# State-space output products of four heads in four column groups, and one unread transpose behind the last

## The chip, the core and the metric

The kernel runs on one core of a Trainium2 chip. The metric is the device time of one execution in microseconds; the time before is the median of three runs. The engines are called by their short names in the rows: PE (TensorE matmul), PEld (TensorE weight load), DVE (VectorE), ACT (ScalarE), POOL (GpSimd), SP (SyncE, which issues most transfers).

## The reference

One decoder layer on 256 tokens of width 2048, in float32. A wide projection feeds sliding-window attention, a diagonal state-space branch and two sigmoid gates; the branches are merged, projected, and followed by a gated feed-forward with a short convolution. The change lies in the state-space branch, whose core is this:

```python
bu = einsum('gph,blgh->blgp', bb, ug)             # complex, 32 groups of 16 channels, 64 states
xs = associative_scan(combine, (ab, bu), axis=1)  # over the 256 tokens
y = (einsum('ghp,blgp->blgh', c_re, xs_re) - einsum('ghp,blgp->blgh', c_im, xs_im)
     + d_skip.reshape(SSM_GROUPS, SSM_GROUP) * ug)
y_val, y_gate = split(gelu(y) @ w_glu + b_glu, 2)
ssm = y_val * sigmoid(y_gate)
```

The two einsums of `y` are the output products of the title.

## The kernel before

Activations stand transposed: channels on the partitions, 256 tokens along the free dimension. All large weights come as units of 128 x 1024 numbers. Each unit is cast by ScalarE into a rounded part `whi`, VectorE subtracts to get the rest `wlo`, and TensorE makes three products of each 128 x 128 block (hi by hi, hi by the activation's rest, lo by hi). The main loop (from line 995) goes through the units in a fixed order: q, u, kv, the gates ga and gs, the attention's output product A, glu, S, the output projection o, then up and dn of the feed-forward. Five units are prepared ahead (`LOOK`), in five buffers.

The attention (`g_attn`, line 631) and the state-space branch (`g_ssm`, line 372) are generators that are woven into this loop. They yield for a VectorE turn ("D") or a ScalarE turn ("A"), or until something is there. `later(fn)` (line 757) puts TensorE work aside until the planner's clock of TensorE, `clk_pe`, has passed a due time; `run_aux` (line 765) issues it between two blocks of the main loop. The planner's clocks are sums of modelled costs (lines 92 to 120); they set the order of the instructions only, and what runs when is then set by semaphores on the chip.

The state-space branch has 16 turns j (`NJ`), each for two groups with 64 states: 128 partitions. They are called heads here; four of them make one block c of 128 output channels. In turn j:

- `va`, `vb` (line 583): VectorE takes the input products `pq[j]` from PSUM and turns them by the powers `E`;
- `products` (line 593) issues on TensorE `y_mm(j - 1, x)`, the output products of the head before, and `pq_mm(j + 1)`, the input products of the next;
- `Z` (line 601): four scans on VectorE;
- `xa`, `xb` (line 617): the states turned back, into `x`, which TensorE reads as float32;
- once in four turns `y_ev(c - 1)` (line 568) adds the skip term and writes the block back into `uY`.

`y_mm` (line 560) makes two products of one head: the stationary `cT` is 128 x 32, so each head uses one column group of 32 columns of the array, and writes 32 partitions of the bank `yps[c]`. A float32 matmul leaves two records in the trace, so a head leaves four. The tile pool gives `T1`, `T2` and `Z` two buffers each, `Sc` and `PT` of the attention one each. After the last head, `g_act` (line 711) applies gelu to `uY` and splits it into `su`, the moving operand of glu; between the two units of glu0 the main loop issues A3x and A3y, the last blocks of the attention's output product. E is built at lines 457 to 501 with work tiles under the tags `T1` and `T2`, by VectorE and, for the last doubling, ScalarE.

Of the kernel before, what the change touches and what calls it, by code (L numbers as in the profile page):

```python
# [8 lines left out]
F32 = mybir.dt.float32  # L9
# [3 lines left out]
ALU = mybir.AluOpType  # L13
AX = mybir.AxisListType

P = 128
T = 256
# [120 lines left out]
def hybrid_block_kernel(  # L138
# [33 lines left out]
    def bank(tag, *dims):  # L172
        banks[0] += 1
        return axp.tile([P, *dims], F32, tag=tag, name=f"{tag}{banks[0]}", bufs=2 if tag == "at" else 1)
# [197 lines left out]
    def g_ssm():  # L372
# [86 lines left out]
        V.memset(E[:, 1, :, 0:1], 0.0)  # L459
        V.tensor_copy(E[:, 0, :, 1:2], cn.unsqueeze(2))  # L460
        V.tensor_copy(E[:, 1, :, 1:2], sn.unsqueeze(2))
        L = 1
        while L < P:
            cnt = L if L < 64 else 63
            jn = min(NJ, 256 // L) if L < 64 else 2
            late = []
            for j0 in range(0, NJ, jn):
                js = slice(j0, j0 + jn)
                a = p1.tile([P, 2, jn, cnt], F32, tag="T1", name=f"ea{L}_{j0}", bufs=2)
                b = p1.tile([P, 2, jn, cnt], F32, tag="T2", name=f"eb{L}_{j0}", bufs=2)  # L470
                lr = E[:, 0:1, js, L : L + 1].to_broadcast([P, 2, jn, cnt])
                li = E[:, 1:2, js, L : L + 1].to_broadcast([P, 2, jn, cnt])
                src = E[:, :, js, 1 : cnt + 1]

                def add(js=js, a=a, b=b):
                    tt(E[:, 0, js, L + 1 : L + 1 + cnt], a[:, 0], b[:, 1], ALU.subtract)
                    tt(E[:, 1, js, L + 1 : L + 1 + cnt], a[:, 1], b[:, 0], ALU.add)

                if L == 64 and j0 // jn % 3 == 2:
                    yield "D", None  # L480
                    tt(a, src, lr, ALU.mult)
                    tt(b, src, li, ALU.mult)
                    add()
                elif L == 64:
                    yield "A", None
                    for j in range(jn):
                        S.activation(a[:, :, j], src[:, :, j], AF.Identity, scale=E[:, 0, j0 + j, L : L + 1])
                        S.activation(b[:, :, j], src[:, :, j], AF.Identity, scale=E[:, 1, j0 + j, L : L + 1])
                    late.append(add)
                    if len(late) == 2:  # L490
                        yield "D", None
                        late.pop(0)()
                else:
                    tt(a, src, lr, ALU.mult)
                    tt(b, src, li, ALU.mult)
                    add()
                    if L >= 8:
                        yield "D", None
            for f in late:
                yield "D", None  # L500
                f()
            L *= 2
# [9 lines left out]
        def z3(a):  # L512
            return a.unsqueeze(2).to_broadcast([P, NJ, 32])

        wa = p1.tile([P, NJ, 32], F32, tag="T1", name="cwa", bufs=2)
        wb = p1.tile([P, NJ, 32], F32, tag="T2", name="cwb", bufs=2)
        tt(wa, cT[:, 0], z3(zi), ALU.mult)
        tt(wb, cT[:, 1], z3(zi), ALU.mult)
        tt(cT[:, 0], cT[:, 0], z3(zr), ALU.mult)
# [37 lines left out]
                    PE.matmul(pq[j][:, ri], B[c][h][rows, i % 2, P * ri : P * ri + P], U[c][rows, i % 2], start=h == 0,  # L557
                              stop=h == 1, tile_position=(r, 0))

        def y_mm(j, x):  # L560
            c, i = j // 4, j % 4
            if i == 0:
                yps[c] = bank("yp", T)
            o = yps[c][32 * i : 32 * i + 32]
            PE.matmul(o, cT[:, 0, j], x[:, 0], start=True, stop=False, tile_position=(0, 32 * i))
            PE.matmul(o, cT[:, 1, j], x[:, 1], start=False, stop=True, tile_position=(0, 32 * i))

        def y_ev(c):
            stt(uY[:, c], uY[:, c], pcol("d", c), yps[c], ALU.mult, ALU.add)
# [10 lines left out]
        for j in range(NJ):  # L580
            c = j // 4
            yield "D", tok
            a = p1.tile([P, 2, 2, P], F32, tag="T1", name=f"va{j}", bufs=2)
            b = p1.tile([P, 2, 2, P], F32, tag="T2", name=f"vb{j}", bufs=2)
            tt(a, pq[j], bE(0, j), ALU.mult)
            tt(b, pq[j], bE(1, j), ALU.mult)
            tt(a[:, 0], a[:, 0], b[:, 1], ALU.add)
            tt(a[:, 1], a[:, 1], b[:, 0], ALU.subtract)
            if j % 4 == 3 and c < 3:
                yield "A", None  # L590
                split_b(c + 1)

            def products(j=j, x=x):
                if j:
                    y_mm(j - 1, x)
                if j + 1 < NJ:
                    pq_mm(j + 1)

            tok = later(products)
            yield "D", None  # L600
            Z = p1.tile([P, 2, 2, P], F32, tag="Z", name=f"z{j}", bufs=2)
            ini = p1.tile([P, 4], F32, tag="ini", name=f"ini{j}", bufs=2)
            mb = mag[:, j : j + 1].to_broadcast([P, P])
            for ri in range(2):
                V.tensor_tensor_scan(Z[:, ri, 0], mb, a[:, ri, 0], 0.0, op0=ALU.mult, op1=ALU.add)
            ts(ini[:, 2:4], Z[:, :, 0, 127], E128[:, 0, j : j + 1], ALU.mult)
            stt(ini[:, 0:1], Z[:, 1, 0, 127:128], E128[:, 2, j : j + 1], ini[:, 2:3], ALU.mult, ALU.add)
            stt(ini[:, 1:2], Z[:, 0, 0, 127:128], E128[:, 1, j : j + 1], ini[:, 3:4], ALU.mult, ALU.add)
            for ri in range(2):
                V.tensor_tensor_scan(Z[:, ri, 1], mb, a[:, ri, 1], ini[:, ri : ri + 1], op0=ALU.mult, op1=ALU.add)  # L610
            if j % 4 == 1 and c < 3:
                yield "A", None
                stage_u(c + 1)
            yield "D", tok
            if j % 4 == 2 and c < 3:
                load_b(c + 1)
            x = p1.tile([P, 2, 2, P], F32, tag="T1", name=f"xa{j}", bufs=2)
            b = p1.tile([P, 2, 2, P], F32, tag="T2", name=f"xb{j}", bufs=2)
            tt(x, Z, bE(0, j), ALU.mult)
            tt(b, Z, bE(1, j), ALU.mult)  # L620
            tt(x[:, 0], x[:, 0], b[:, 1], ALU.subtract)
            tt(x[:, 1], x[:, 1], b[:, 0], ALU.add)
            if j % 4 == 0 and j:
                y_ev(c - 1)
                st[f"y{c - 1}"] = True
        yield "D", later(lambda: y_mm(NJ - 1, x))
        y_ev(3)
        st["y3"] = True

# [1 line left out]
    def g_attn():  # L631
# [40 lines left out]
        for i in range(8):  # L672
            if i == 4:
                yield "A", wait_for("q1")
            yield "D", later(lambda: scores(i))
            Sc = p1.tile([P, 2, 3, P], F32, tag="Sc", name=f"sc{i}")
            n6 = p1.tile([P, 2, 3], F32, tag="n6", name=f"n6_{i}", bufs=2)
            nm = p1.tile([P, 2, 2], F32, tag="nm", name=f"nm{i}", bufs=2)
            sm = p1.tile([P, 2, 2], F32, tag="sm", name=f"sm{i}", bufs=2)
            es = p1.tile([P, 2, 2], F32, tag="es", name=f"es{i}", bufs=2)  # L680
            nsb = nsink[:, 2 * i : 2 * i + 2].unsqueeze(2).to_broadcast([P, 2, 2])
            for h in range(2):
                V.scalar_tensor_tensor(out=Sc[:, h], in0=dist.rearrange("p (s k) -> p s k", s=3),
                                       scalar=-SLOPES[i + 8 * h], in1=ps[h], op0=ALU.mult, op1=ALU.add)
            V.tensor_reduce(n6, Sc, AX.X, ALU.max, negate=True)
            V.tensor_tensor(n6[:, :, 1:2], n6[:, :, 1:2], n6[:, :, 2:3], op=ALU.min)
            V.tensor_tensor(nm, n6[:, :, 0:2], nsb, op=ALU.min)
            V.tensor_tensor(es, nm, nsb, op=ALU.subtract)
            yield "A", None
            for h in range(2):  # L690
                S.activation(Sc[:, h, 0], Sc[:, h, 0], AF.Exp, bias=nm[:, h, 0:1], accum_out=sm[:, h, 0:1])
                S.activation(Sc[:, h, 1:3], Sc[:, h, 1:3], AF.Exp, bias=nm[:, h, 1:2], accum_out=sm[:, h, 1:2])
            S.activation(es, es, AF.Exp)
            yield "D", None
            V.tensor_tensor(sm, sm, es, op=ALU.add)
            V.reciprocal(sm, sm)
            yield "A", None
            for h in range(2):
                S.activation(Sc[:, h, 0], Sc[:, h, 0], AF.Identity, scale=sm[:, h, 0:1])
                S.activation(Sc[:, h, 1:3], Sc[:, h, 1:3], AF.Identity, scale=sm[:, h, 1:2])  # L700
            yield "A", later(lambda: turn(Sc))
            PT = p1.tile([P, 2, 3, P], F32, tag="PT", name=f"pt{i}")
            for h in range(2):
                S.copy(PT[:, h], ps[h])
            yield "A", later(lambda: values(PT))
            S.copy(ath[:, i], ps[0])
            yield "D", None
            V.tensor_tensor(atl[:, i], ps[0], ath[:, i].bitcast(F32), op=ALU.subtract)
# [509 lines left out]
```

## Time and profile before

| | us |
|---|---|
| runs: lowest, median, highest | 1214.19, 1214.31, 1218.68 |
| profiled execution | 1220.22 |
| its span, first to last instruction | 1218.4 |
| TensorE busy in the span | 1204.8 |
| VectorE busy | 825.9 |
| ScalarE busy | 600.2 |
| mean granted clock of TensorE | 0.996 |

The time of the profiled execution is its span and 1.8 us around it. Matmuls are pipelined and the ends of their records are modelled, so their busy time is not work at full rate; the distance from one start to the next says more. A row of the chain gives the time from the end of one step to the end of the next.

### The profile page before, as it was taken

How to read it: one execution, taken by the hardware profiler on the slowest of the kernel's cores; microseconds unless marked ns; L12 is line 12 of the kernel's file. 1: busy time of each engine (PE TensorE's matmuls, PEld its weight loads, DVE VectorE, ACT ScalarE, POOL GpSimd, SP SyncE). 2: the span in 40 equal slices, each digit the busy share in tenths (PEclk: the TensorE clock that was granted, in tenths of full speed). 3: DMA queues.
4: the chain of work that ended last, by engine and by line, in shares of the span. 5: the costliest groups of instructions: out<-in, count | busy, mean ns of one | idle time of the engine just before them, and what ended most of it. 6: DMA issues, size and time to landing. Idle time of an engine off the chain costs nothing.

```text
span 1218.4 us, 24557 instructions
## 1 busy us (share of the span) xinstructions
PE 1204.8 (99%) x10348; PEld 1181.8 (97%) x10348; DVE 825.9 (68%) x1172; ACT 600.2 (49%) x817; POOL 10.4 (1%) x24
## 2 busy tenths in 40 slices
PE   9999999999999999999999999999999999999996
PEld 9999999899999999999999999999999999999996
DVE  6987898989978655666666666666666644454543
ACT  7667555555435444644545445454454534343541
POOL 0000000000000000000000000000000000000000
PEclk9999999999999999999999999999999999999998
DMA  8755545455556666466565665646556575656561
GB/s 303 231 190 189 165 146 165 156 153 160 166 161 180 237 207 188 156 223 193 180 209 166 224 191 178 212 165 225 191 182 205 167 225 177 208 183 208 178 190 69
DMA packets 64911, 228.53 MB, mean 188 GB/s; under 512 B 7648, under 2 KB 9056, under 8 KB 64672
## 3 DMA queue, kind: packets, MB, share of 16 engines
q1 hardware_dynamic: 63648, 223.55, 56.6%
q0 software_dynamic: 1152, 3.41, 0.9%
q8 instruction: 81, 1.33, 0.4%
q14 instruction: 30, 0.25, 0.1%
HBM read 224.31 MB, written 2.10 MB: 186 GB/s over the span
## 4 chain that ended last, share of the span: by engine, by line
PE 98%; DVE 1%; DMA 0%; ACT 0%; SPq 0%; issue 0%; DVEq 0%
PE acc_up L132 39%; PE acc_dn L132 19%; PE acc_gs L132 7%; PE acc_ga L132 7%; PE acc_o L132 7%; PE acc_q L132 3%; PE acc_A L132 3%; PE pq L132 2%; PE at L132 2%; PE acc_u L132 2%; PE acc_S L132 2%; PE yp L132 1%; PE acc_glu L132 1%; PE aux L132 1%; DMA raw<-in_wst_dram 0%; DVE xo_sq L132 0%
## 5 line engine op out<-in xcount | busy, mean ns | idle before, releaser
L132 DVE TENSOR_TENSOR wlo<-raw,whi 128x1024 fp32r<-128x1024 f32 (+2 forms) x421 | 503.1, 1210 | 313.2 <-ACT whi L132 312.1
L132 ACT CAST whi<-raw 128x1024 fp32r<-128x1024 f32 (+2 forms) x421 | 432.9, 1041 | 454.4 <-PE acc_up L132 145.9
L132 PE MATMUL acc_up<-x2g,whi 128*128 128x256 f32 x2816 | 479.6, 276 | 0.0
L132 PEld LDWEIGHTS acc_up<-x2g,whi 128*128 128x128 f32 x2816 | 424.2, 188 | 0.0
L132 PE MATMUL acc_up<-x2g,wlo 128*128 128x256 f32 x1408 | 388.8, 276 | 0.0
L132 PEld LDWEIGHTS acc_up<-x2g,wlo 128*128 128x128 f32 x1408 | 264.5, 188 | 0.0
L132 PE MATMUL acc_dn<-H,whi 128*128 128x256 f32 x1384 | 235.7, 276 | 0.0
L132 PEld LDWEIGHTS acc_dn<-H,whi 128*128 128x128 f32 x1384 | 208.3, 188 | 0.0
L132 PE MATMUL acc_dn<-H,wlo 128*128 128x256 f32 x692 | 191.1, 276 | 0.0
L132 PEld LDWEIGHTS acc_dn<-H,wlo 128*128 128x128 f32 x692 | 129.9, 188 | 0.0
L132 PE MATMUL acc_gs<-xg,whi 128*128 128x256 f32 x512 | 90.7, 281 | 0.0
L132 PE MATMUL acc_ga<-xg,whi 128*128 128x256 f32 x512 | 90.7, 281 | 0.0
L132 PEld LDWEIGHTS acc_ga<-xg,whi 128*128 128x128 f32 x512 | 77.3, 188 | 2.8 <-issue 2.0
L132 PEld LDWEIGHTS acc_gs<-xg,whi 128*128 128x128 f32 x512 | 77.4, 188 | 2.6 <-issue 1.7
L132 PE MATMUL acc_o<-mh,whi 128*128 128x256 f32 x256 | 71.9, 281 | 0.0
L132 PE MATMUL acc_o<-ml,whi 128*128 128x256 f32 x256 | 71.9, 281 | 0.0
L132 PE MATMUL acc_o<-mh,wlo 128*128 128x256 f32 x256 | 71.9, 281 | 0.0
L132 PE MATMUL acc_ga<-xg,wlo 128*128 128x256 f32 x256 | 71.0, 277 | 0.0
L132 PE MATMUL acc_gs<-xg,wlo 128*128 128x256 f32 x256 | 71.0, 277 | 0.0
L132 PEld LDWEIGHTS acc_o<-mh,wlo 128*128 128x128 f32 x256 | 49.2, 192 | 0.0
L132 PEld LDWEIGHTS acc_ga<-xg,wlo 128*128 128x128 f32 x256 | 48.1, 188 | 0.0
L132 PEld LDWEIGHTS acc_gs<-xg,wlo 128*128 128x128 f32 x256 | 48.1, 188 | 0.0
(204 smaller groups left out, 1312.7 us busy)
## 6 DMA issues: line engine op xcount, KB each, us to landing
raw<-in_wst_dram SPq DMA_DIRECT2D x415, 512.0 KB, 4.2
xres<-in_xT_dram POOLq DMA_DIRECT2D x1, 2048.0 KB, 9.9
x_in<-in_xT_dram SPq DMA_DIRECT2D x7, 256.0 KB, 6.0
out_dram<-xo_sq SPq DMA_DIRECT2D x7, 256.0 KB, 2.4
br<-in_ssmb_dram POOLq DMA_DIRECT2D x3, 256.0 KB, 5.3
raw<-in_wst_dram SPq DMA_DIRECT2D x2, 256.0 KB, 3.2
cT<-in_ssmc_dram SPq DMA_DIRECT2D x1, 512.0 KB, 6.2
us<-ul POOLq DMA_DIRECT2D x16, 32.0 KB, 3.6
```

What stands on the lines that cost most here:

```text
L132: return fn(*a, **k)
```

## The change

The output products of four heads are issued together, in turns j = 4, 8, 12 and at the end, instead of one head a turn. Within such a batch the real parts of the four heads come first, each in its own column group, then the four imaginary parts. For this the states of four heads are kept: `x` becomes a tile of four heads under the tag `X4`, with one buffer, whose place the work tiles of E use before it (`W4`, in two halves). To make room, `T1`, `T2` and `Z` get one buffer instead of two, and `PT` goes into the buffer of `Sc`. After the last batch TensorE transposes `ident` once into a bank that nobody reads.

```diff
+        W4 = p1.tile([P, 4, 512], F32, tag="X4", name="w4")
...
-                a = p1.tile([P, 2, jn, cnt], F32, tag="T1", name=f"ea{L}_{j0}", bufs=2)
-                b = p1.tile([P, 2, jn, cnt], F32, tag="T2", name=f"eb{L}_{j0}", bufs=2)
+                a, b = [W4[:, 2 * (turns % 2) + i, 0 : 2 * jn * cnt].rearrange("p (r j n) -> p r j n", r=2, j=jn)
+                        for i in range(2)]
+                turns += 1
...
-        def y_mm(j, x):
-            c, i = j // 4, j % 4
-            if i == 0:
-                yps[c] = bank("yp", T)
-            o = yps[c][32 * i : 32 * i + 32]
-            PE.matmul(o, cT[:, 0, j], x[:, 0], start=True, stop=False, tile_position=(0, 32 * i))
-            PE.matmul(o, cT[:, 1, j], x[:, 1], start=False, stop=True, tile_position=(0, 32 * i))
+        def y_mm(c, x):
+            yps[c] = bank("yp", T)
+            for ri in range(2):
+                for i in range(4):
+                    PE.matmul(yps[c][32 * i : 32 * i + 32], cT[:, ri, 4 * c + i], x[:, i, ri], start=ri == 0,
+                              stop=ri == 1, tile_position=(0, 32 * i), skip_group_check=True)
+
+        def y_last(x):
+            y_mm(3, x)
+            PE.transpose(bank("at", P), ident, ident)
...
-            a = p1.tile([P, 2, 2, P], F32, tag="T1", name=f"va{j}", bufs=2)
-            b = p1.tile([P, 2, 2, P], F32, tag="T2", name=f"vb{j}", bufs=2)
+            a = p1.tile([P, 2, 2, P], F32, tag="T1", name=f"va{j}")
+            b = p1.tile([P, 2, 2, P], F32, tag="T2", name=f"vb{j}")
...
-                if j:
-                    y_mm(j - 1, x)
+                if j and j % 4 == 0:
+                    y_mm(j // 4 - 1, x)
...
-            Z = p1.tile([P, 2, 2, P], F32, tag="Z", name=f"z{j}", bufs=2)
+            Z = p1.tile([P, 2, 2, P], F32, tag="Z", name=f"z{j}")
...
-            x = p1.tile([P, 2, 2, P], F32, tag="T1", name=f"xa{j}", bufs=2)
-            b = p1.tile([P, 2, 2, P], F32, tag="T2", name=f"xb{j}", bufs=2)
-            tt(x, Z, bE(0, j), ALU.mult)
+            if j % 4 == 0:
+                x = p1.tile([P, 4, 2, 2, P], F32, tag="X4", name=f"x{c}")
+            b = p1.tile([P, 2, 2, P], F32, tag="T2", name=f"xb{j}")
+            xj = x[:, j % 4]
+            tt(xj, Z, bE(0, j), ALU.mult)
...
-        yield "D", later(lambda: y_mm(NJ - 1, x))
+        yield "D", later(lambda: y_last(x))
...
-            PT = p1.tile([P, 2, 3, P], F32, tag="PT", name=f"pt{i}")
+            PT = p1.tile([P, 2, 3, P], F32, tag="Sc", name=f"pt{i}")
```

## Rows read from the trace of the kernel before

**Rows 1.** The page: busy time of each engine (share of the span, number of records), and the chain of work that ended last by engine.

```profile
PE 1204.8 (99%) x10348; PEld 1181.8 (97%) x10348; DVE 825.9 (68%) x1172; ACT 600.2 (49%) x817; POOL 10.4 (1%) x24
...
PE 98%; DVE 1%; DMA 0%; ACT 0%; SPq 0%; issue 0%; DVEq 0%
```

**Rows 2.** Busy time by stage from 140 to 362 us: the sum over the stages (us of time, then busy us of each engine).

```profile
sum 222.00, PE 222.00 PEld 203.11 DVE 195.60 ACT 109.12 POOL 7.55; mean PE 55.50 PEld 50.78 DVE 48.90 ACT 27.28 POOL 1.89
```

**Rows 3.** Who waited for whom from 140 to 362 us: us in total, times, longest us.

```profile
ACT whi L132 <- PE acc_gs L132: 33.3, 21, 3.6
...
ACT whi L132 <- PE acc_ga L132: 21.7, 11, 4.6
ACT whi L132 <- PE acc_A L132: 20.2, 10, 3.6
...
DVE wlo L132 <- ACT whi L132: 14.0, 15, 1.5
```

**Rows 4.** The chain that ended last in order of time (start us, us, what), 100 to 360 us: the first, the eighth and the last of the sixteen steps on `yp`, which all have the same length.

```profile
141.17 0.98 PE yp L132 x4
...
250.18 0.98 PE yp L132 x4
...
357.64 0.98 PE yp L132 x4
```

**Rows 5.** Timeline of TensorE around the fourth head's products (start us, us to the end of the last of the group, what, number).

```profile
186.75 0.28 PE L132 MATMUL acc_ga<-xg,wlo 128*128 128x256 f32 x1
186.95 1.05 PE L132 MATMUL yp<-xa,cT 128*32 128x256 f32 x4
187.94 0.38 PE L132 MATMUL pq<-us,bh 64*128 64x256 f32 x1
...
188.60 0.50 PE L132 MATMUL acc_ga<-xg,whi 128*128 128x256 f32 x2
```

**Rows 6.** Timeline of TensorE where the first input products `pq` stand alone.

```profile
122.30 0.28 PE L132 MATMUL acc_ga<-xg,wlo 128*128 128x256 f32 x1
122.51 0.38 PE L132 MATMUL pq<-us,bh 64*128 64x256 f32 x1
```

**Rows 7.** The same timeline as in rows 5 in windows that end after the first, the second and the third record of `yp`.

```profile
186.95 0.40 PE L132 MATMUL yp<-xa,cT 128*32 128x256 f32 x1
...
186.95 0.62 PE L132 MATMUL yp<-xa,cT 128*32 128x256 f32 x2
...
186.95 0.83 PE L132 MATMUL yp<-xa,cT 128*32 128x256 f32 x3
```

**Rows 8.** Timeline of TensorE, the attention's value products (`values`, two column groups of 64), in windows that end after the first, the second and the fourth record.

```profile
97.86 0.43 PE L132 MATMUL at<-pt,vtok 128*64 128x256 f32 x1
...
97.86 0.44 PE L132 MATMUL at<-pt,vtok 128*64 128x256 f32 x2
...
97.86 0.65 PE L132 MATMUL at<-pt,vtok 128*64 128x256 f32 x4
```

**Rows 9.** TensorE by stage, in stretches of full-array matmuls alone: window, its length, busy us (number of records that touch it), granted clock, DMA share, GB/s.

```profile
168.30:172.80 4.50, 4.50 (x42) 1.00 0.65 215
...
221.00:232.00 11.00, 11.00 (x99) 1.00 0.47 144
...
288.00:293.50 5.50, 5.50 (x51) 1.00 0.56 147
...
323.00:334.00 11.00, 11.00 (x96) 1.00 0.48 153
360.00:378.00 18.00, 18.00 (x155) 1.00 0.53 155
384.00:490.00 106.00, 106.00 (x903) 1.00 0.63 204
500.00:1190.00 690.00, 690.00 (x6090) 1.00 0.60 193
```

**Rows 10.** Timeline of TensorE at the first six transposes of the attention.

```profile
93.01 0.82 PE L132 MATMUL at<-ident,sc 128*128 128x128 f32 x6
93.59 0.48 PE L132 MATMUL acc_ga<-xg,whi 128*128 128x256 f32 x2
```

**Rows 11.** The chain in order of time where TensorE waits between glu and the end of S.

```profile
373.90 4.61 PE acc_S L132 x39
...
380.84 1.14 DVE tS L132
...
382.11 11.54 PE acc_S L132 x96
```

**Rows 12.** The bank `at`: the products that spread the second norm's factor (duration min/median/max in ns, first and last start in us).

```profile
L132 PE MATMUL at<-dg,ones x8: 271/274/275, 47.0 to 499.2; 128*128 128x128 f32 x8
```

**Rows 13.** Timeline of VectorE, the first `xa` of the third block.

```profile
252.32 0.66 DVE L132 TENSOR_TENSOR xa<-z,E 128x512 f32<-128x512 f32 x1
```

**Rows 14.** Timeline of VectorE and TensorE from the last head's block to the second half of glu0.

```profile
358.66 0.48 DVE L132 SCALAR_TENSOR_TENSOR uY<-uY,pr,yp 128x256 f32<-128x256 f32 x1 [0.90 <-PE yp L132]
...
360.07 0.43 DVE L132 TENSOR_TENSOR su<-uY,su 128x256 fp32r<-128x256 f32 x1 [0.92 <-ACT su L132]
...
361.48 0.40 PE L132 MATMUL acc_glu<-su,whi 128*128 128x256 f32 x2
```

More of the change, by code (lines that the diff above doesn't have):

```diff
@@ L461, in g_ssm @@
         V.tensor_copy(E[:, 1, :, 1:2], sn.unsqueeze(2))
-        L = 1
+        L, turns = 1, 0
+        W4 = p1.tile([P, 4, 512], F32, tag="X4", name="w4")
         while L < P:
@@ L513, in z3 @@
             return a.unsqueeze(2).to_broadcast([P, NJ, 32])
-        wa = p1.tile([P, NJ, 32], F32, tag="T1", name="cwa", bufs=2)
-        wb = p1.tile([P, NJ, 32], F32, tag="T2", name="cwb", bufs=2)
+        wa = p1.tile([P, NJ, 32], F32, tag="T1", name="cwa")
+        wb = p1.tile([P, NJ, 32], F32, tag="T2", name="cwb")
         tt(wa, cT[:, 0], z3(zi), ALU.mult)
@@ L616, in g_ssm @@
                 load_b(c + 1)
-            x = p1.tile([P, 2, 2, P], F32, tag="T1", name=f"xa{j}", bufs=2)
-            b = p1.tile([P, 2, 2, P], F32, tag="T2", name=f"xb{j}", bufs=2)
-            tt(x, Z, bE(0, j), ALU.mult)
+            if j % 4 == 0:
[3 more added lines that the diff above has]
+            tt(xj, Z, bE(0, j), ALU.mult)
             tt(b, Z, bE(1, j), ALU.mult)
-            tt(x[:, 0], x[:, 0], b[:, 1], ALU.subtract)
-            tt(x[:, 1], x[:, 1], b[:, 0], ALU.add)
+            tt(xj[:, 0], xj[:, 0], b[:, 1], ALU.subtract)
+            tt(xj[:, 1], xj[:, 1], b[:, 0], ALU.add)
             if j % 4 == 0 and j:
```

## Prediction

> **What bounds the kernel now.** I read the page first. TensorE is busy 99% of the span, and 98% of the chain that ended last is TensorE's [rows 1]. So a nanosecond taken from TensorE is a nanosecond off the end, as long as nobody else becomes late. Next the stage in which the change lies: the state-space products run from 141.17 to 358.6 us [rows 4], and between 140 and 362 us TensorE has no idle time at all while VectorE works 195.6 of 222 us [rows 2]. Third, who waits there: ScalarE's casts wait for TensorE to give weight buffers back, 75 us in the three largest groups, and VectorE's subtractions wait for those casts [rows 3]. The two feeding engines are ahead and are held back by TensorE; no TensorE wait on them appears in this stretch.
>
> **The change: the column groups.** Today each head costs one insertion on the chain: four records, 0.98 us, sixteen times [rows 4], so 15.68 us. Inside it the records follow each other at 0.22 us: one record ends 0.40 us after the start, two 0.62, three 0.83, and four 1.05 [rows 5, 7]. A full-array record before it takes 0.11 us. The step into the products is 0.20 us (186.75 to 186.95) instead of 0.11 [rows 5]; a step into the `pq` products alone is 0.21 (122.30 to 122.51) [rows 6]. So when a y insertion in front of a `pq` insertion goes away, the entry cost stays and the whole 0.98 us goes. Twelve of sixteen insertions go: 12 x 0.98 = 11.76 us.
>
> What the remaining four cost depends on overlap. The trace has no four groups side by side, but it has two: the attention's value products alternate between columns 0 and 64. There one record ends 0.43 us after the start and a second one 0.01 us later; four end at 0.65 [rows 8], where four in one group end at 1.05 [rows 5]. Two groups so run in the time of one, each pair's second start costing next to nothing; the first pair is 0.03 us longer than one record of the state-space products (0.43 against 0.40). A batch of four heads has sixteen records in four groups, four deep as one head is now. Bounds: 0.98 us if four groups overlap as two do; 16 x 0.215 + 0.12 = 3.56 if they don't at all (0.12 is what 0.98 holds beyond four steps). I take the nearer row, the pairs, and add 3 x 0.03 for three neighbours: 1.07 us a batch, 4.28 for four. Saving: 15.68 - 4.28 = 11.4 us.
>
> The Trainium skill, "TensorE: Matmul & The Clock Gate", Part 3 (Measured speedup vs the span model), reports 3.07 times for four row tiles, not 4. By that ratio the products would cost 15.68 / 3.07 = 5.1 us and the saving would be 10.6 us, 0.8 us less than by the rows; no run shown here has four groups.
>
> **The turn of ident.** One 128-wide transpose: six of them, with the step out, fill 93.01 to 93.59 [rows 10], about 0.1 us each. Bounds 0 (it replaces part of a mode step) and 0.3 (a step of its own of 0.2 on top); I take 0.1. It goes to a buffer of `at` that was free long ago. But transposes do something else. The full-array matmuls have two steps in this trace, at the same granted clock (1.00, the 2.4 GHz level). A window's records, less the 2.4 that straddle its edge, give 113.3 ns (500 to 1190 us: 690 / 6087.6) or 117.7 ns (384 to 490: 106 / 900.6) [rows 9]. After the transposes the step is the short one: 4.5 / 39.6 = 113.6 in 168.3 to 172.8, 5.5 / 48.6 = 113.2 in 288 to 293.5, and so behind all eight sets. After the value products it is the long one, and products of `yp` and `pq` mostly keep the step that they find (117.5 in 323 to 334, 113.9 in 221 to 232) [rows 9]. After the last y insertion it is 118.0 (360 to 378) and stays long until the `dg` products at 499.2 us [rows 9, 12]. From 358.6 to 499.2 us, less 0.9 of waiting at 381 [rows 11], are 139.7 / 0.1177 = 1187 records; at 4.4 ns each the turn is worth 5.2 us if the short step lasts until 499. It has to survive one wait: TensorE stands from 381.2 to 382.1 us for `tS`, VectorE's reading of an accumulator [rows 11]. No short step is seen to cross such a wait in this stage; if it falls there, the gain is only 22.6 / 0.1177 x 4.4 ns = 0.85 us. I take the whole, since the step changes in this trace mostly where the form of the matmul changes.
>
> In the middle stage the twelve products of `pq` that now stand alone may turn the step too. By the chain in order of time about 110 us of the stage stand behind such products, half of it at either step today, and 4.4 of 117.7 ns are 3.7%: bounds -2.1 and +2.1 us (55 x 3.7%), and I take 0.
>
> **What is hidden.** The single buffers of `T1`, `T2` and `Z` are written and read by VectorE alone, in order: nothing is late. `W4` keeps two halves, as two buffers did. `PT` in `Sc`'s buffer makes ScalarE's first copy wait for the last transpose instead of the third, at most 0.33 us eight times, covered by ScalarE's 75 us of waiting for TensorE [rows 3]; uncovered it would be 2.6 us. The one wait that matters is `x`: the first xa of a four waits for the batch before it. That place exists today: `yp` of 250.18 ends by 251.2, xa starts at 252.32 [rows 4, 13]. The batch is 0.1 us longer, so the wait stays hidden by 1 us; behind it VectorE's queue holds the next weight subtraction. VectorE's cover shrinks: 195.6 us of work in 222 - 11 = 211 us is 93%, still under 100. At the end the last y must pass uY and su (358.66 to 360.5 us) before the second half of glu0 at 361.5 [rows 14]; the planner counts 1.3 us less before it and so may place it about 12 records later, but glu0's first twelve records there don't read that part. I take 0, at most 1 us.
>
> **Sum.** On the profiled execution, 1220.22 us (span 1218.4 and 1.8 around it): -11.4 + 0.1 - 5.2 = 1203.7. The median of the runs, 1214.31, is 5.9 us lower, and one of the three runs is 4.4 us above the other two: about what the long step from 358 to 499 us costs. If the median's runs had the short step there, the change takes only 11.3 from them: 1203.0. The two meet, and I predict 1203.5 us.
>
> **Rivals.** (a) The groups overlap, but the short step dies at the wait of 382 us: 1220.2 - 11.3 - 0.85 = 1208.1. For it: the long step before the wait is the long one after it, so the wait restarts something unknown; against it: two of three runs are already low.
>
> (b) Groups overlap only partly: two at a time gives 8 x 0.215 + 0.12 = 1.84 us a batch, 7.4 in all, saves 8.3 in place of 11.4, and 3.1 on top of the forecast is 1206.6. If a matmul's two records had to finish issue before the next group's, a batch would have nine slots, 2.06 us, saves 7.4, and the time would be 1207.5. Against both: in the pairs the second record to start came 0.01 us after the first, not a slot later [rows 8]. The Trainium skill, "TensorE: Matmul & The Clock Gate", Part 3 (The mechanism), has matmuls start strictly first in, first out; that speaks for the nine slots and their 1207.5, and the pairs speak against it.
>
> (c) The change doesn't do what it says: no overlap among four groups, 4 x 3.56 = 14.2, saves 1.4 less 0.1: 1213.0 from the median. For it only that four groups are unseen.
>
> (d) Slower: each change of group empties the array as a change of form does, (0.20 - 0.11) before and 0.11 behind, 0.2 us [rows 5], for each of 16 x 4 records: +12.8 on (c), 1225.8. It takes 0.12 us per change to pass 1220.4; the pairs show 0.01 [rows 8].
>
> **Chances.** The forecast 0.62, (a) 0.13, (b) 0.13, (c) 0.09, (d) 0.03. 0.5% of 1214.31, 6.1 us, is about what a measurement can tell from no change: 1208.2 and 1220.4 are the limits. The forecast, (b) and a third of (a) are faster by more: 0.79; the rest of (a) and (c): 0.18; (d): 0.03. Range: the forecast with its middle-stage bounds (1201.4 to 1205.6), a batch at its cheapest and the low end of the step's play reach 1199.5; upward it takes in (a) and (b) with 1.4 us for their own play, 1209.5. (c), (d) and some tails stay out, under 2 in 10.
>
> **What the profile would show.** Right: `yp` in four insertions of 16 records, about 1.07 us each on the chain; 0.98 us gone in front of twelve `pq`s; a step of 113 ns from the turn to 499 us; TensorE still without idle time in the stage. Wrong: batches of 1.8 us or more (b, c, d); 118 ns after 382 us (a); waits of TensorE for wlo between 140 and 350 us, which would mean VectorE's cover is gone; a wait for su in front of glu0's second half.

## The result

The changed kernel took 1203.26 us (median; 1201.95 to 1205.58), the kernel before 1215.25 beside it. The ratio is 0.9898 with a 95% interval of 0.9878 to 0.9917: 12.4 us less by the ratio, between 10.1 and 14.8 (the two medians lie 12.0 apart). The executions of either kernel lie at two levels, and on both sides two of the six are at the upper one (1218.7 and 1219.1 before, 1205.3 and 1205.6 now), so the difference doesn't come from another mix of the two. The prediction was 1203.5 us, 1199.5 to 1209.5, faster. The number came out; one of the two terms that made it did not, and the experiments were needed to see that. As in the prediction, the turn is the unread transpose, and the step is the time from the start of one full-array matmul to the start of the next, short (113 ns) or long (118 ns).

The profiled execution of the changed kernel took 1202.64 us, with a span of 1200.9. The page, as in [rows 1]:

```profile
PE 1187.4 (99%) x10349; PEld 1172.6 (98%) x10349; DVE 824.6 (69%) x1172; ACT 600.3 (50%) x817; POOL 10.4 (1%) x24
...
PE 98%; DVE 1%; DMA 0%; ACT 0%; SPq 0%; issue 0%; DVEq 0%
```

TensorE has the same number of records but one (the unread transpose) and is still the bound. The chain in order of time, 100 to 360 us (compare [rows 4]), with two of the `pq` insertions, the four batches and what follows the last:

```profile
122.42 0.67 PE pq L132 x4
...
174.22 0.66 PE pq L132 x4
185.70 1.00 PE yp L132 x16
186.70 0.67 PE pq L132 x4
...
247.13 1.00 PE yp L132 x16
...
301.33 1.00 PE yp L132 x16
...
347.14 1.00 PE yp L132 x16
348.14 0.26 PE at L132
348.40 0.35 PE pq L132 x3
```

Sixteen records now take 1.00 us where four took 0.98. The products cost 4.0 us where they cost 15.7. A `pq` insertion costs 0.66 to 0.67 with or without y in front of it (`pq` behind the last batch is other work, the three last products of A3y). How the batch starts stands in the timeline of TensorE, in windows that end after the second, fourth, fifth and sixteenth record (compare [rows 7, 8]):

```profile
185.63 0.41 PE L132 MATMUL yp<-x,cT 128*32 128x256 f32 x2
...
185.63 0.42 PE L132 MATMUL yp<-x,cT 128*32 128x256 f32 x4
...
185.63 0.62 PE L132 MATMUL yp<-x,cT 128*32 128x256 f32 x5
...
185.63 1.07 PE L132 MATMUL yp<-x,cT 128*32 128x256 f32 x16
```

Four records end within 0.02 us of each other, the fifth 0.2 us later (one slot): four groups run side by side as two did. Busy time by stage from 140 to 350 us, the sum (compare [rows 2]), and TensorE's only wait from 100 to 400 us:

```profile
sum 210.00, PE 210.00 PEld 199.14 DVE 194.57 ACT 109.34 POOL 7.56; mean PE 52.50 PEld 49.78 DVE 48.64 ACT 27.34 POOL 1.89
```

```profile
PE acc_S L132 <- DVE tS L132: 0.7, 1, 0.7
```

VectorE is at 93% and TensorE doesn't wait for it. The last question is the step of the full-array matmuls behind the last batch. TensorE by stage, as in [rows 9], of the changed kernel:

```profile
383.00:473.00 90.00, 90.00 (x796) 1.00 0.66 220
500.00:1170.00 670.00, 670.00 (x5915) 1.00 0.60 195
```

With 2.4 records at the edge taken off, 383 to 473 us has 90 / 793.6 = 113.4 ns; the kernel before had 117.7 in the stretch that holds the same work [rows 9]. So this profile looks as if the turn had done what the sum gave it 5.2 us for.

### The profile page after: what moved, and what is told of

Same layout as the page of the kernel before. It is cut to its first block, busy times and chain, and to the rows that moved or that the text cites. A ratio compares the mean times of both kernels' runs of the same rounds, so it can differ in the third digit from the quotient of the medians.

```text
span 1200.9 us, 24567 instructions
## 1 busy us (share of the span) xinstructions
PE 1187.4 (99%) x10349; PEld 1172.6 (98%) x10349; DVE 824.6 (69%) x1172; ACT 600.3 (50%) x817; POOL 10.4 (1%) x24
## 4 chain that ended last, share of the span: by engine, by line
PE 98%; DVE 1%; DMA 0%; ACT 0%; SPq 0%; issue 0%; DVEq 0%
PE acc_up L132 40%; PE acc_dn L132 20%; PE acc_gs L132 8%; PE acc_ga L132 8%; PE acc_o L132 7%; PE acc_q L132 3%; PE acc_A L132 3%; PE pq L132 2%; PE at L132 2%; PE acc_u L132 2%; PE acc_S L132 2%; PE acc_glu L132 1%; PE aux L132 1%; DMA raw<-in_wst_dram 0%; DVE xo_sq L132 0%; PE yp L132 0%
## 5 line engine op out<-in xcount | busy, mean ns | idle before, releaser
L132 DVE TENSOR_TENSOR wlo<-raw,whi 128x1024 fp32r<-128x1024 f32 (+2 forms) x421 | 503.0, 1210 | 303.0 <-ACT whi L132 302.2
L132 PEld LDWEIGHTS acc_o<-mh,whi 128*128 128x128 f32 x256 | 48.0, 188 | 0.0
```

The source lines that it names most:

```text
L132: return fn(*a, **k)
```

## The experiments

Each kernel was timed beside the kernel before on the same chip.

**The turn taken away, and the turn alone.** The changed kernel without the transpose:

```diff
         def y_last(x):
             y_mm(3, x)
-            PE.transpose(bank("at", P), ident, ident)
```

> The changed kernel without the unread transpose behind the last batch. Theory (the transpose sets the short step of 113 ns behind it): what follows the last batch is left to chance, as behind the two lone y insertions of the kernel before, of which one was followed by the short step and one by the long; in executions with the long step of 117.8 ns over some 1,130 records up to the second norm the time is 4.7 us higher, so about 1207.5 us, in the others 1203. Rival (the transpose does nothing, the short step there comes from the batch): 1203 us in all, short step in the profile. The y batches stay at 1.00 us by both.

And the kernel before with the transpose behind its last y insertion:

```diff
-        yield "D", later(lambda: y_mm(NJ - 1, x))
+        def y_last(x):
+            y_mm(NJ - 1, x)
+            PE.transpose(bank("at", P), ident, ident)
+
+        yield "D", later(lambda: y_last(x))
```

> The kernel before with nothing but the unread transpose behind its last y insertion. Theory: its low executions (1214 to 1215) already had the short step from 358 to 499 us, its high ones (1219) the long one; the transpose gives the short step always, so the median stays at 1214 to 1215 us and the executions near 1219 are gone. Rival: all its executions had the long step there, as the profiled one did; then the median falls by 4.7 us to about 1210 us.

Without the turn: 1203.01 us (1202.20 to 1207.34), ratio 0.9888 (0.9866 to 0.9910), the same as with it. The turn alone: 1215.66 us (1213.12 to 1218.89) against 1215.67, ratio 0.9992 (0.9977 to 1.0007), and the executions near 1219 are still there: five of twelve above 1217, where the kernel before has eight of seventeen. The turn is worth nothing that these times can tell; the interval leaves room for 2.8 us, not for 5.2. The median did not fall to 1210 us either, as the rival of the second run had it. TensorE by stage far behind the turn in the two profiles, without the turn and with the turn alone:

```profile
383.00:473.00 90.00, 90.00 (x766) 1.00 0.65 213
```

```profile
383.00:473.00 90.00, 90.00 (x797) 1.00 0.64 214
```

90 / 763.6 = 117.9 ns without it, 90 / 794.6 = 113.3 with it: for these two the step goes with the turn, while the times say that it is not the turn's doing. The next run shows which is true. What the turn does do is seen right behind it. The run with the turn alone, in two stretches behind its transpose at 358.1 us:

```profile
358.60:371.60 13.00, 13.00 (x117) 1.00 0.51 156
372.20:380.00 7.80, 7.80 (x69) 1.00 0.64 216
```

The first has 13 / 114.6 = 113.4 ns, where the kernel before had 118.0 [rows 9], the second 7.8 / 66.6 = 117.1. So the turn does set the short step behind the last y, and it is lost some 14 us later, still ahead of the wait for `tS`. By the starts of the records, all six profiles with the turn in this place have the short step right behind it, and all eight without it the long one. The turn costs little: without it the three `pq` products behind the batch take 0.55 us on the chain, with it 0.26 + 0.35.

```profile
347.99 0.55 PE pq L132 x3
```

**Head by head.** The two products of a head in a row, in the same batch, turn kept:

```diff
-            for ri in range(2):
-                for i in range(4):
+            for i in range(4):
+                for ri in range(2):
```

> The changed kernel with the two products of a head issued one behind the other (head outside, real and imaginary part inside) in the same batch. Theory (matmuls are issued in order, and one whose column group is occupied holds up those behind it): a head's second product overlaps only with the next head's first; ten slots of 0.215 us and 0.12, 2.27 us a batch, 5.1 us more in all, about 1208 us. Rival (the groups take their work independently of the order): 1.00 us a batch and 1203 us. Second rival (no overlap at all this way): 3.56 us a batch, 1213 us.

1202.49 us (1201.81 to 1207.00), ratio 0.9884 (0.9864 to 0.9905). The chain in order of time, first and last batch:

```profile
185.67 1.02 PE yp L132 x16
...
347.18 1.02 PE yp L132 x16
```

The first rival was right, my theory and the second rival wrong: a batch took 1.02 us where the theory had 2.27, so here a product that waits for its own group doesn't hold up the next group's. The order of the change (real parts first) is worth 0.02 us a batch, nothing. The same profile has the turn and, behind it, the long step:

```profile
383.00:473.00 90.00, 90.00 (x766) 1.00 0.64 211
```

**Pairs.** Eight batches of two heads, turn kept:

```diff
-        def y_mm(c, x):
-            yps[c] = bank("yp", T)
+        def y_mm(k, x):
+            c = k // 2
+            if k % 2 == 0:
+                yps[c] = bank("yp", T)
             for ri in range(2):
-                for i in range(4):
+                for i in range(2 * k % 4, 2 * k % 4 + 2):
...
-                if j and j % 4 == 0:
-                    y_mm(j // 4 - 1, x)
+                if j and j % 2 == 0:
+                    y_mm(j // 2 - 1, x)
```

> The changed kernel with batches of two heads instead of four (eight batches of eight records, the turn kept). Theory (an insertion is four slots long whatever the number of groups): eight insertions of 0.98 to 1.0 us, 8 us in place of 4, so 4 us more, about 1207 us. Rival (a batch costs by its records): 0.5 us each, no change, 1203 us.

1207.09 us (1205.86 to 1211.98), ratio 0.9924 (0.9903 to 0.9946): 4.1 us more than the version without the turn beside it (1203.01) and 4.6 more than head by head (1202.49), which has the turn; 4 were expected. The chain in order of time, first and last of eight:

```profile
154.32 0.99 PE yp L132 x8
...
349.83 0.99 PE yp L132 x8
```

An insertion is 0.98, 0.99 or 1.00 us long with one, two or four groups. So the gain on the chain is the number of insertions: 16 to 8 saves 7.8 us, 16 to 4 saves 11.7.

**What draws the step.** In these traces the step behind the last batch mostly changes at places where TensorE waits or nearly waits: a delay of 0.15 us inside glu0's second half, one of 0.04 us early in S, and the wait for `tS`, 0.96 us from start to start. The last two in the timeline of the changed kernel:

```profile
359.31 0.39 PE L132 MATMUL acc_S<-sy,whi 128*128 128x256 f32 x2
...
359.65 0.44 PE L132 MATMUL acc_S<-sy,whi 128*128 128x256 f32 x2
...
368.05 0.28 PE L132 MATMUL acc_S<-sy,wlo 128*128 128x256 f32 x1
369.01 0.47 PE L132 MATMUL acc_S<-sy,whi 128*128 128x256 f32 x2 [0.68 <-DVE tS L132]
```

And its step in front of the first of the two, and between them, 8.8 / 77.6 = 113.4 and 8 / 67.6 = 118.3 ns:

```profile
350.60:359.40 8.80, 8.80 (x80) 1.00 0.49 135
360.00:368.00 8.00, 8.00 (x70) 1.00 0.65 211
```

So in the changed kernel the turn's short step was gone before the wait, and the short step from 383 to 473 us begins behind the wait. To test this, the transpose was moved behind that wait, to the front of the output projection, or the wait was removed by letting VectorE read S0 before it prepares the next unit, or both (with the transpose moved, the one behind the batch is left out):

```diff
+        if name == "o0" and k0 == 0:
+            PE.transpose(bank("at", P), ident, ident)
         mh, ml = mover(name)
```

```diff
             held.append((name, acc))
+            if name == "S0":
+                drain()
         prep(i + LOOK)
```

> The changed kernel with the unread transpose moved from behind the last y batch to the front of the output projection, behind the last wait of TensorE before the second norm. Theory (a transpose sets the short step, and the waits at glu and S draw it anew, so that behind y it is lost): the some 900 records from the output projection to the second norm have the short step in every execution; the profile shows 113 ns there, the executions near 1206 us are gone, and the median falls by at most 1 us to 1202 to 1203 us. Rival (the step behind 370 us is chance whatever comes before): 1203 us with executions at 1206 to 1207 as before.

> The changed kernel, turn kept behind the last batch, with VectorE's reading of the accumulator of S0 put ahead of the next weight unit's preparation, so that TensorE need not wait for it. Theory (that wait draws the step anew): the wait of 0.85 us is gone and the step keeps what the short waits at the start of S left, the long one in all profiles so far; time 1206 us in all executions (0.85 less, 4.1 more than the low ones). Rival (the wait has nothing to do with the step): 0.85 us less and the same two levels, 1202 and 1206 us.

> Both edits: VectorE's reading of S0 first, and the transpose at the front of the output projection instead of behind the last y batch. Theory: the wait of 0.85 us is gone and the step is short from there to the second norm in every execution; 1201 to 1202 us, none above 1204. Rival (the step is chance): low level 1201 to 1202 and high level 1206.

> As the kernel with both edits, and an unread transpose behind the value products of the attention's sixth and eighth pair of heads, where some 350 records with the long step follow in the changed kernel's profile. Theory: 350 x 4.2 ns less two transposes of 0.11 us, 1.2 us less than with both edits alone, about 1200.2 us. Rival (one transpose doesn't hold its step through the products that follow): no gain, 0.2 us more.

On that chip the kernel before took 1219.48 us, all seven executions at its upper level (1217.68 to 1220.50), so these ratios come out lower than those of the other runs; the times of the four versions among themselves say more, at four executions each. The transpose in front of the output projection: 1203.34 us, but from 1201.30 to 1207.07, ratio 0.9873 (0.9851 to 0.9894); the spread that it should have ended is there. S0 first: 1205.60 us (1203.87 to 1206.20), 0.9885, not the 1206 in all executions that were expected. Both: 1204.70 us (1204.35 to 1205.20), 0.9881. Two further turns in the attention: 1205.32 us (1205.06 to 1205.57), 0.9886, so nothing gained by them either. With S0 first the chain in order of time has no wait left in S (compare [rows 11]):

```profile
355.28 22.55 PE acc_S L132 x192
377.83 7.18 PE acc_o L132 x61
```

And the step from there to the second norm is the long one in the three profiles of these versions that have no wait, with the transpose at the output projection or without; here S0 first alone, then both, then with the two further turns:

```profile
361.00:367.00 6.00, 6.00 (x53) 1.00 0.59 180
383.00:473.00 90.00, 90.00 (x767) 1.00 0.62 207
```

```profile
383.00:473.00 90.00, 90.00 (x767) 1.00 0.62 206
```

```profile
383.00:473.00 90.00, 90.00 (x767) 1.00 0.63 208
```

So half of the theory held. Without the wait the step of S is kept, and one transpose in a stream of full-array matmuls doesn't change it; the executions with both edits lie within 0.9 us, which fits. The other half, that a transpose sets the short step wherever it stands, fell. Removing a wait of 0.85 us made the kernel no faster: in the profiles it also took away the place at which the step can become short again. The step behind S is not all that moves an execution. The lowest one with S0 first, 1203.87 us, is the profiled one and has the long step there; its records from 12 to 41 us have the shorter step (29 / 253.6 = 114.4 ns, against 29 / 246.6 = 117.6 in the changed kernel's profile), which over some 300 records is worth 1.3 us.

**Six in a row.** The attention always has six, and the short step behind them. S0 first, and six transposes in front of the output projection:

```diff
         if name == "o0" and k0 == 0:
-            PE.transpose(bank("at", P), ident, ident)
+            room = bank("at", 3, P)
+            for r in range(6):
+                PE.transpose(room[:, r % 3], ident, ident)
```

> As the kernel with S0 read first, but with six unread transposes in a row at the front of the output projection in place of one, as the attention has them. Theory (six in a row set the short step where one does not): 849 records of the output projection and the first up unit at 113 ns in place of 118, 3.6 us less, for 0.6 us of transposes: 3 us under the version with one transpose, at one level, 1201 to 1202 us. Rival (transposes don't set the step in the middle of full-array matmuls): 0.5 us more than with one transpose, 1205 us.

> The changed kernel itself once more, beside the one with six transposes. Theory: two levels some 4 us apart, about 1202 and 1206 us, by the step that the wait at S leaves; its profile shows the one or the other behind the wait. No other theory is told apart by this run; it gives the base for the run beside it.

1205.35 us (1202.69 to 1206.40), ratio 0.9909 (0.9890 to 0.9927); the changed kernel beside it 1202.72 us (1201.38 to 1206.31), 0.9893 (0.9872 to 0.9913). That is 2.6 us over the changed kernel, and no less than S0 first alone on the other chip (1205.60), so the six gave nothing that the median shows. The profiled execution, though, was the lowest of its kind, 1202.69 us, with the short step. So two more executions of it were profiled:

> The version with six transposes in front of the output projection, once more for its profile: its timed executions lie near 1205.4 us while the profiled one took 1202.7 with the short step behind the six. Theory (six set the step): an execution near 1205 shows the short step there all the same and has lost its time elsewhere. Rival (they don't): it shows the long step from the six to the second norm.

> The same once more, for a second profile: short step behind the six by the theory, long step in an execution near 1205 us by the rival.

They took 1205.31 and 1202.66 us. TensorE by stage before and behind the six, first in the execution of 1202.69 us, then in that of 1205.31:

```profile
370.00:377.50 7.50, 7.50 (x66) 1.00 0.53 152
383.00:473.00 90.00, 90.00 (x797) 1.00 0.65 218
```

```profile
370.00:377.50 7.50, 7.50 (x68) 1.00 0.57 170
383.00:473.00 90.00, 90.00 (x767) 1.00 0.63 205
```

In the first the step goes from 7.5 / 63.6 = 117.9 to 113.3 ns across the six, in the second from 7.5 / 65.6 = 114.3 to 117.7; the execution of 1202.66 us does as the first. The six turned the step over in all three; they set nothing. None of the versions is clearly faster than the changed kernel.

## Why the prediction was right

**The column groups: right, mechanism and size.** Predicted 1.07 us a batch and 11.4 us saved; measured 1.00 and 11.7. The row taken, two groups in the value products [rows 8], carried over to four, with less for the neighbours than the 0.03 each that was added: the first four records end 0.02 us apart. The ratio of 3.07 that the Trainium skill, "TensorE: Matmul & The Clock Gate", Part 3 (Measured speedup vs the span model), gives for four row tiles would have meant 10.6 us; the trace has 15.7 / 4.0 = 3.9. Of the rivals, partial overlap (b) is out by four records within 0.02 us, and its nine slots for issue in order by the head-by-head run as well (1.02 us); (c) and (d) are out by the same rows. The version without the turn has the whole gain, and the pairs lose the part that their eight insertions cost, so the gain is the batches' and not the turn's.

**The turn: wrong.** The step of the sum that failed is "the turn is worth 5.2 us if the short step lasts until 499", and with it the reason given, that "the step changes in this trace mostly where the form of the matmul changes". The turn did set the short step behind the last y, but in the changed kernel's profile it was long again from the delay of 0.04 us at 359.8. Even the delay in glu0, 0.15 us at 350.1 here, can end it: there the step went from long to short without the turn, and from short to long head by head. The turn alone kept it for 118 records, 0.5 us at 4.4 ns each. The cost of the turn was about right: 0.06 us net on the chain (0.26 + 0.35 against 0.55) where 0.1 was taken.

Rival (a) had the better mechanism: the wait at S draws the step anew. But (a) priced it as a loss for every execution. Of the eight profiles with this wait, three have the long step behind it (before, no turn, head by head) and five the short one (changed kernel twice, turn alone, pairs, transpose at the output projection), with the turn and without it, before and after the change. The three are executions at the upper level of their kernel and the five are not. That single executions of one kernel differ in this way is read from the two levels in their times; two profiles of one kernel that differ there exist only for the version with six transposes, which has no such wait.

**Why the number held.** The sum had two legs. The one on the profiled execution (1203.7) held by luck: that profile of before has the long step from 358 to 499 us, and the profile of after drew the short one at the wait. The one on the median (1203.0) was the better one: it gave the turn nothing and so needed only the column groups. Its condition, that the median's executions had the short step already, fits their time, but no profile of the kernel before at 1214 us shows it. The turn alone showed that the median of before had nothing to gain from the turn: 1215.66 against 1215.67. The measured 12.4 us, 10.1 to 14.8, agree with 11.7 less 0.06.

Of the 17.5 us between the two spans 11.7 less 0.06 are the batches and the turn, and 4.1 are the step from the wait at S (369 us) to the second norm (476): 107 / 0.1134 records times 4.3 ns. By the starts of the records the changed kernel's profile also has 120 fewer records at the long step between the last batch and the wait, and 125 fewer from 100 us to the last batch, 0.5 us each. The rest, under 1 us, is not placed.

**What was hidden: right, but for a wait that was named as a sign of being wrong.** VectorE at 93% as computed, no TensorE wait on wlo, none on the single `x`. Not tried: the single buffers apart from the batches. The last y moved by more than the twelve records forecast: three records of A3y follow it where 24 did. So glu0's second half waits for `su`: its first thirteen records run on time, and the fourteenth starts at 350.12 us, 0.05 us after VectorE has made the rest of the last `su` (349.64 + 0.43). In all ten profiles with such a delay the late record starts 0.05 to 0.06 us behind that end. The price was inside the "at most 1 us": 0.15 us in all. VectorE's row, and the timeline of TensorE there, where two records take 0.55 us in place of 0.40:

```profile
349.64 0.43 DVE L132 TENSOR_TENSOR su<-uY,su 128x256 fp32r<-128x256 f32 x1 [0.92 <-ACT su L132]
```

```profile
349.62 0.39 PE L132 MATMUL acc_glu<-su,whi 128*128 128x256 f32 x2
349.85 0.28 PE L132 MATMUL acc_glu<-su,wlo 128*128 128x256 f32 x1
349.96 0.55 PE L132 MATMUL acc_glu<-su,whi 128*128 128x256 f32 x2
350.34 0.28 PE L132 MATMUL acc_glu<-su,wlo 128*128 128x256 f32 x1
```

**The middle stage: within its bounds.** The forecast was 0 within 2.1 us (55 x 3.7% is 2.0). Behind `pq` products that stand alone the step is sometimes the short one and sometimes the long one; the 125 records above make it 0.5 us less in this pair of profiles.

## What to carry to other kernels

Small products that use a quarter of the array's columns are best kept until four of them, one for each column group, can go together: in this kernel the insertion then cost what one cost, and the order within it made 0.02 us. Before a difference between one profile and another is given to a change, ask whether the same difference stands between two executions of one kernel; a sum made against a profiled execution should be made against the median too, and where the two need different terms, one of the terms is doubtful. An edit that is meant to steer such a difference is tested alone, on the old kernel.

## What was not expected of the hardware

Full-array matmuls of 256 columns run at 113.3 to 113.6 or at 117.7 to 118.0 ns a step, at the same granted clock of 1.00 (the 2.4 GHz level), and the step can be kept for hundreds of records. It was drawn anew at the wait of 0.96 us and at delays of 0.15 and 0.04 us, kept where the wait was removed, short behind one transpose that follows the y products, kept across one transpose in a stream of full-array matmuls, and turned over by six. What decides it stays open. From the wait at S to the second norm it is worth about 4 us of 1,203, a third of what this change brought.
